# Twelve decay products, eight merge additions and 28 residual additions of a hybrid decoder layer, from GpSimd to DVE

## The chip, the cores and the metric

The kernel runs on one core of a Trainium2 chip. TensorE (PE in the profile) multiplies matrices, DVE is the vector engine, ScalarE (ACT) applies functions and copies, GpSimd (POOL) is a slower, programmable vector engine, and SyncE (SP) issues most DMAs. The metric is the device time in microseconds, from the median of several runs; one further execution was profiled.

## The reference

One layer of a decoder runs over 512 prompt rows and 32 sampled rows (8 sequences of 4). Cut to what the change touches:

```python
h = h + 0.5 * rmsnorm(swiglu(u, ffn1...), ffn1_post_g)          # residual addition behind a norm
z, xbc, dt, q, k, v, qi, ki, wi, g_ssd, g_att = split(rmsnorm(h) @ w_in)
...
decay  = exp(where(causal, a_cs[t] - a_cs[s], -inf))             # SSD, chunks of 128
cb     = einsum('bctgn,bcsgn->bctsg', cc, bc)                    # C B, one for a group of 4 heads
y_diag = einsum('bctsgr,bcsgrp->bctgrp', cb[..., None] * decay, xdt)
...
merged = sigmoid(g_ssd) * (y_ssd @ w_br_ssd) + sigmoid(g_att) * (y_att @ w_br_att)
h = h + rmsnorm(merged @ w_out, mix_post_g)                      # residual addition behind a norm
h = h + rmsnorm(mem_attend(rmsnorm(h)) @ w_mo, mem_post_g)       # the same
h = h + 0.5 * rmsnorm(swiglu(rmsnorm(h), ffn2...), ffn2_post_g)  # the same
```

There are 32 SSD heads in 8 groups, and the model width is 1024.

## The kernel before

All activations lie transposed: channels on the 128 partitions, 544 columns of tokens (512 prompt, 32 sample). A matrix product is made of three passes of fp32r (high by high, low by high, high by low; L310, accumulators `pg` and `pgh`), so every weight tile `wr` that lands is split by ScalarE into `wh` (L270) and by DVE into the rest `wl` (L271). The stages follow one another: ffn1, the mixing stage (first the indexer and the attention of the prompt, then the SSD groups 0 to 7 beside the selection and attention of the sample), the merge with w_out, the attention over the memory with w_mo, and ffn2. Side tasks are woven between the large products by hand (`weave`), and a scheduler of the build then puts each engine's instructions in order, so a change of one engine's work moves neighbours on others too.

Three places use GpSimd for an instruction with two full tensor operands:

- **SSD, `ssd_y`, L1380.** For each group and each half i (two heads), ScalarE turns the broadcast sums `abc` into decays (eight Relu of 128 columns, L1377, one Exp over 1024, L1379). Then `abc` is multiplied by `cb`, the masked C B that DVE has made from PSUM (L1353). GpSimd has this product, but for i = 1 in groups 1 to 4, where DVE has it: 12 on GpSimd, 4 on DVE. The products are read much later by `pY` (L1501). Around it DVE makes the convolution of the group that follows (`XO`, three multiply-adds L1326 and one L1329 for each of four tiles, whose inputs are in SBUF), `xd` and `xe` (L1368, L1370, from the transposes `pxt` in PSUM), and then a row of short ones (`cbs`, `xds`, `Gs`, `xef`, `Bs`).
- **Merge, L1761.** For each of eight output tiles m, DVE multiplies the accumulator by the gate (`gt`, L1760) and GpSimd adds the attention's part `y`. ScalarE then makes the high half `uh` and DVE the low half `ul` for w_out.
- **Norms, `bound`, L386.** Behind a norm, for each k of 8 tiles, DVE scales `y` (L385) and then `y` is added to the residual `hT`: on DVE for even k, on GpSimd for odd k. ScalarE squares the sum (L369), and GpSimd adds the square into `sqh` (L370; the last of eight is on DVE), from which TensorE makes the row sums `sth` for the norm that follows. `bound` runs for each half of the columns (256, 288) while the other half's products run; seven runs of it have a residual addition, so there are 28 such additions on GpSimd.

GpSimd also issues the gathers of the sampled attention (`kv`, L1618) and makes the low halves `wl` of the gates' weights.

Of the kernel before, what the change touches and what calls it, by code (L numbers as in the profile page):

```python
# [13 lines left out]
ALU = mybir.AluOpType  # L14
# [3 lines left out]
P = 128  # L18
T = 544
TP = 512  # L20
# [83 lines left out]
def weave(*gens, extra=(), loose=()):  # L104

    now, idle = 0.0, 0
    live = [[g, 0.0] for g in (*gens, *extra)]
    ends = [g for g in gens if g not in loose]  # L110
    while any(x[0] in ends for x in live):
        s = next((x for x in live if x[1] <= now), None)
        if s is None:
            s = min(live, key=lambda x: x[1])
            now = s[1]
        try:
            v = next(s[0])
        except StopIteration:
            live.remove(s)
            idle = 0  # L120
            continue
        if v is WAIT:
            idle += 1
            assert idle < 10000, "a wait that nothing ends"
            s[1] = now + 0.3
            continue
        idle = 0
        c, d = v if isinstance(v, tuple) else (v or 0.0, 0.0)
        now += c
        s[1] = now + d  # L130
# [38 lines left out]
class Net:  # L169
# [202 lines left out]
    def bound(self, half, sq, post_g, pre_g, rt=None):  # L372


        nc, hT, y = self.nc, self.hT, self.y
        r0, n = HALF[half]
        sl = slice(r0, r0 + n)
        if post_g is not None:
            yield 0.0, 3.0
            r = yield from self.rms_h(sq, half)  # L380
        if pre_g is not None:
            acc = self.nw.tile([P, 288], F32, tag="sqh", name="sqh", bufs=2)
        for k in range(8):
            if post_g is not None:
                nc.vector.scalar_tensor_tensor(y[:, k, sl], y[:, k, sl], post_g[:, k:k + 1], r, op0=ALU.mult, op1=ALU.mult)  # L385
                (nc.gpsimd if k % 2 else nc.vector).tensor_tensor(hT[:, k, sl], hT[:, k, sl], y[:, k, sl], op=ALU.add)  # L386
            if pre_g is not None:
                self.sq_acc(acc, hT[:, k, sl], n, k == 0, last=(k == 7))
            if rt is not None:
                g = pre_g[:, k:k + 1]  # L390
                nc.scalar.activation(self.uh[:, k, sl], hT[:, k, sl], AF.Copy, scale=g)
                nc.vector.scalar_tensor_tensor(self.ul[:, k, sl], hT[:, k, sl], g, self.uh[:, k, sl].bitcast(F32), op0=ALU.mult, op1=ALU.subtract)
            yield 0.0, 1.0
        if pre_g is None:
            return
        yield 0.0, 4.0 if rt is None else 8.0
        r = yield from self.rms_h(acc, half)
        if rt is not None:
            nc.scalar.copy(rt[:, sl], r)
            return  # L400
        for k in range(8):
            u = self.nw.tile([P, 288], F32, tag="u", name="u", bufs=2)
            nc.vector.scalar_tensor_tensor(u[:, :n], hT[:, k, sl], pre_g[:, k:k + 1], r, op0=ALU.mult, op1=ALU.mult)
            self.split(self.uh[:, k, sl], self.ul[:, k, sl], u[:, :n], nc.gpsimd if k % 4 == 3 else None)
            yield 0.0, 0.9
# [932 lines left out]
    def ssd_y(self, g, z):  # L1338
        nc, I, O, sp = self.nc, self.I, self.O, self.sp
# [3 lines left out]
        abc = []  # L1343
# [8 lines left out]
        cb = sp.tile([P, 4, P], F32, tag="cb", name="cb")  # L1352
# [20 lines left out]
        for i in range(2):  # L1373
            for h in range(2):
                for c in range(4):
                    col = c * 32 + 4 * g + 2 * i + h
                    nc.scalar.activation(abc[i][:, h, c * P:(c + 1) * P], abc[i][:, h, c * P:(c + 1) * P], AF.Relu, scale=-1.0,  # L1377
                                         bias=self.acs[:, col:col + 1])
            nc.scalar.activation(abc[i], abc[i], AF.Exp, scale=-1.0)  # L1379
            (nc.vector if 1 <= g <= 4 and i else nc.gpsimd).tensor_tensor(abc[i], abc[i], cb.rearrange("p c t -> p (c t)").unsqueeze(1).broadcast_to([P, 2, TP]), op=ALU.mult)  # L1380

        ps = self.ps1("pcs")
        for q in range(3):
# [106 lines left out]
        for i in range(2):  # L1490
# [14 lines left out]
            y = sp.tile([P, T], F32, tag=f"y{i}", name=f"y{i}")  # L1505
            nc.vector.scalar_tensor_tensor(y[:, :TP], XO[i][:, :TP], self.dsk[:, tl:tl + 1], ps, op0=ALU.mult, op1=ALU.add)
            nc.vector.tensor_tensor(y[:, P:TP], y[:, P:TP], E, op=ALU.add)
            t = sp.tile([P, 32], F32, tag="ty", name="ty")
# [229 lines left out]
    def merge(self, h_d, rest):  # L1738

        nc, I, y = self.nc, self.I, self.y  # L1740
        ex = ExitStack()
        ep = self.pool("mg", ex)
        ys = []

        def load():
            for k in range(16):
                yt = ep.tile([P, T], F32, tag="yt", name="yt", bufs=3)
                nc.sync.dma_start(yt, self.yssd_d[k])
                yh = ep.tile([P, T], F32R, name=f"yh{k}")
                yl = ep.tile([P, T], F32R, name=f"yl{k}")  # L1750
                self.split(yh, yl, yt)
                ys.append((yh, yl))
                yield 0.0, 2.0

        weave(rest, load())
        for m in range(8):
            w = self.weights(("w_br_ssd", m), [I["w_br_ssd"][0][:, m * P:(m + 1) * P]], 16)
            t = self.gate(0, m, ep)
            ps = result(self.mm(w, ys, 0))
            nc.vector.tensor_tensor(t, ps, t, op=ALU.mult)  # L1760
            nc.gpsimd.tensor_tensor(t, t, y[:, m, :], op=ALU.add)  # L1761
            self.split(self.uh[:, m, :], self.ul[:, m, :], t)
        ex.close()
        self.open_h()
        nc.sync.dma_start(self.hT, h_d.rearrange("k p t -> p k t"))
# [280 lines left out]
def result(gen):  # L2046

    while True:
        try:
            next(gen)  # L2050
        except StopIteration as e:
            return e.value
# [32 lines left out]
```

## Time and profile before

| | |
|---|---|
| median of 3 runs (lowest, highest) | 2201.06 us (2200.52, 2204.1) |
| the profiled execution, and its span | 2201.23 us, 2199.4 us |
| TensorE busy | 2101.4 us of the span |
| DVE, ScalarE, GpSimd busy | 1324.2, 955.2, 444.4 us |
| mean granted clock of TensorE | 0.979 |

The span runs from the first to the last instruction of the program. A busy time counts an instruction from its start to its end, also while it is held up. The granted clock is 1.0 where TensorE runs at 2.4 GHz and 0.5 where it runs at 1.2 GHz.

### The profile page before, as it was taken

The page shows a single profiled execution, that of the slowest core. Times are in us where ns is not written, and L with a number is a line of the kernel's source. Part 1 is how long each engine was busy: PE and PEld are TensorE (multiplying, and loading weights), DVE is VectorE, ACT ScalarE, POOL GpSimd, SP SyncE. Part 2 cuts the span into 40 slices and gives each one's busy share as a digit, 9 for nine tenths or more (in the row PEclk, how much of TensorE's full clock was granted, in tenths as well). Part 3 has the DMA queues.
Part 4 walks back from the last instruction along what each step waited for, and adds up shares of the span by engine and source line. Part 5 has one row for each costly group of instructions (what it writes and reads, how often), then busy time and mean ns, then how long its engine had stood idle before and what let it go on. Part 6 is the DMA issues. An engine that isn't in the chain of part 4 may idle for free.

```text
span 2199.4 us, 41232 instructions
## 1 busy us (share of the span) xinstructions
PE 2101.4 (96%) x16675; PEld 1960.6 (89%) x16675; DVE 1324.2 (60%) x2711; ACT 955.2 (43%) x1821; POOL 444.4 (20%) x461
## 2 busy tenths in 40 slices
PE   7999999999999999998999999999999979999998
PEld 7999999998788678897888889999987879999998
DVE  6543334475697989896677668544563475424455
ACT  6323345345445665453556445323535443222233
POOL 0000011032122302225555641012320320000011
PEclk9999999999999999998999999999999999999999
DMA  6424565347442223355456636564443433233243
GB/s 199 126 82 128 165 203 197 113 133 213 135 127 83 88 77 110 117 157 161 126 174 192 178 106 186 175 190 155 144 149 139 154 115 115 76 96 90 81 131 100
DMA packets 320107, 301.70 MB, mean 137 GB/s; under 512 B 25416, under 2 KB 290632, under 8 KB 318868
## 3 DMA queue, kind: packets, MB, share of 16 engines
q1 hardware_dynamic: 310508, 272.58, 40.5%
q0 software_dynamic: 8448, 25.18, 3.7%
q8 instruction: 131, 2.15, 0.4%
q10 hardware_dynamic: 960, 1.31, 0.2%
q14 instruction: 60, 0.49, 0.1%
HBM read 261.14 MB, written 37.35 MB: 136 GB/s over the span
## 4 chain that ended last, share of the span: by engine, by line
PE 72%; DVE 13%; DMA 6%; ACT 4%; issue 3%; POOL 2%; SPq 0%; DVEq 0%; ACTq 0%; POOLq 0%
PE pg L310 42%; PE pgh L310 14%; PE pmo L591 2%; DVE wl L271 2%; ACT wh L270 2%; DMA wr<-in_ffn_wu 1%; DVE gtm L1077 1%; DVE XO L1326 1%; DMA yt<-yssd_d 1%; DMA abc<-ac_d 1%; PE pmkT L1811 1%; POOL sqh L370 1%; PE pmo L1878 1%; DVE XO L1329 1%; DMA wr<-in_ffn_wg 1%
## 5 line engine op out<-in xcount | busy, mean ns | idle before, releaser
L270 ACT CAST wh<-wr 128x1024 fp32r<-128x1024 f32 (+3 forms) x362 | 341.6, 959 | 512.1 <-PE pg L310 288.2
L271 DVE TENSOR_TENSOR wl<-wr,wh 128x1024 fp32r<-128x1024 f32 (+3 forms) x338 | 391.1, 1171 | 222.6 <-ACT wh L270 215.8
L310 PE MATMUL pg<-uh,wh 128*128 128x256 f32 (+1 forms) x2336 | 504.1, 297 | 0.8 <-DVE zt L1291 0.8
L310 PE MATMUL pg<-ul,wh 128*128 128x256 f32 (+1 forms) x2336 | 493.4, 292 | 0.0
L310 PE MATMUL pg<-uh,wl 128*128 128x256 f32 (+1 forms) x2336 | 491.6, 291 | 0.0
L310 PEld LDWEIGHTS pg<-uh,wh 128*128 128x128 f32 x2336 | 380.4, 191 | 21.2 <-issue 17.2
L310 PEld LDWEIGHTS pg<-ul,wh 128*128 128x128 f32 x2336 | 381.2, 191 | 2.9 <-issue 2.2
L310 PEld LDWEIGHTS pg<-uh,wl 128*128 128x128 f32 x2336 | 380.0, 190 | 1.8 <-issue 1.4
L310 PE MATMUL pgh<-uh,wh 128*128 128x288 f32 (+2 forms) x880 | 260.8, 299 | 9.5 <-ACT wh L270 6.1
L310 PE MATMUL pgh<-uh,wl 128*128 128x256 f32 (+2 forms) x880 | 260.3, 298 | 7.3 <-DVE wl L271 7.3
L310 PE MATMUL pgh<-ul,wh 128*128 128x256 f32 (+1 forms) x880 | 257.1, 294 | 0.0
L310 PEld LDWEIGHTS pgh<-uh,wh 128*128 128x128 f32 (+1 forms) x880 | 170.4, 195 | 13.2 <-ACT wh L270 7.0
L310 PEld LDWEIGHTS pgh<-uh,wl 128*128 128x128 f32 (+1 forms) x880 | 169.5, 193 | 11.1 <-DVE wl L271 10.1
L310 PEld LDWEIGHTS pgh<-ul,wh 128*128 128x128 f32 x880 | 171.4, 195 | 0.9 <-issue 0.8
L370 POOL TENSOR_TENSOR sqf<-sqf,sqt 128x256 f32<-128x256 f32 (+1 forms) x48 | 52.4, 1092 | 508.9 <-ACT sqt L369 508.6
L310 PE MATMUL pgh<-hh,wh 128*128 128x288 f32 (+1 forms) x352 | 101.9, 290 | 0.0
L310 PE MATMUL pgh<-hh,wl 128*128 128x288 f32 (+1 forms) x352 | 101.2, 288 | 0.3 <-DVE wl L271 0.3
L310 PE MATMUL pgh<-hl,wh 128*128 128x288 f32 (+1 forms) x352 | 101.4, 288 | 0.0
L1326 DVE SCALAR_TENSOR_TENSOR XO<-CB,convw,XO 128x600 f32<-128x600 f32 x96 | 86.2, 899 | 7.1 <-ACT XO L1324 6.6
L702 POOL DMA_INDIRECT G<-in_cache_kidx,ix x16 | 16.4, 1025 | 361.7 <-DVE ix L697 281.2
L617 DVE TENSOR_TENSOR g<-pg,rt 128x544 f32<-128x544 f32 x32 | 23.2, 725 | 101.1 <-PE pg L310 101.1
L620 DVE TENSOR_TENSOR g<-pg,g 128x544 f32<-128x544 f32 x32 | 23.2, 725 | 99.1 <-PE pg L310 99.1
(608 smaller groups left out, 3875.4 us busy)
## 6 DMA issues: line engine op xcount, KB each, us to landing
wr<-in_w_in SPq DMA_DIRECT2D x66, 512.0 KB
wr<-in_ffn_wg SPq DMA_DIRECT2D x48, 512.0 KB
wr<-in_ffn_wu SPq DMA_DIRECT2D x48, 512.0 KB
wr<-in_ffn_wd SPq DMA_DIRECT2D x44, 384.0 KB
wr<-in_ffn_wd SPq DMA_DIRECT2D x44, 320.0 KB
kt_d<-KT SPq DMA_DIRECT2D x8, 1024.0 KB
KT<-kt_d SPq DMA_DIRECT2D x16, 512.0 KB
wr<-in_w_in SPq DMA_DIRECT2D x32, 256.0 KB
```

Source lines behind the costliest of these rows:

```text
L270: nc.scalar.copy(hi[:, s], r)
L271: (lo_eng or nc.vector).tensor_tensor(lo[:, s], r, hi[:, s].bitcast(F32), op=ALU.subtract)
L310: nc.tensor.matmul(o, a[:, k, c0:c0 + m], x[:, r0:r0 + n], start=(k == 0 and j == 0), stop=(k == KT - 1 and j == 2))
L370: (nc.vector if last else nc.gpsimd).tensor_tensor(acc[:, :n], acc[:, :n], s[:, :n], op=ALU.add)
L591: nc.tensor.matmul(ps[:, :256], a[:, k, i * P:(i + 1) * P], b[:, k, :], start=(k == 0 and j == 0), stop=(k == 7 and j == 2))
L617: nc.vector.tensor_tensor(g1[:, :n], pg, rt[:, sl], op=ALU.mult)
L620: nc.vector.tensor_tensor(g1[:, :n], pu, g1[:, :n], op=ALU.mult)
L1077: nc.vector.scalar_tensor_tensor(G, S, thr[:, j:j + 1], one, op0=ALU.is_ge, op1=ALU.mult, accum_out=cnt[:, j:j + 1])
L1326: nc.vector.scalar_tensor_tensor(xo, CB[:, j:j + 600], cw(j), xo, op0=ALU.mult, op1=ALU.add)
L1329: nc.vector.scalar_tensor_tensor(xo, th, 1.0, xo, op0=ALU.add, op1=ALU.mult)
L1811: nc.tensor.transpose(ps[:, (z * 2 + i) * P:(z * 2 + i + 1) * P], mk[:, i, (k + z) * P:(k + z + 1) * P], self.ident)
L1878: nc.tensor.matmul(ps[:, d * 256:(d + 1) * 256], mv[:, x, h * 256 + d * P:h * 256 + (d + 1) * P], PT[:, x, :], start=(x == 0), stop=(x == 1))
```

## The change

All 12 products, all 8 merge additions and all 28 residual additions of GpSimd are made by DVE. The operands, the arithmetic and the code's order are the same.

```diff
@@ -383,7 +383,7 @@
         for k in range(8):
             if post_g is not None:
                 nc.vector.scalar_tensor_tensor(y[:, k, sl], y[:, k, sl], post_g[:, k:k + 1], r, op0=ALU.mult, op1=ALU.mult)
-                (nc.gpsimd if k % 2 else nc.vector).tensor_tensor(hT[:, k, sl], hT[:, k, sl], y[:, k, sl], op=ALU.add)
+                nc.vector.tensor_tensor(hT[:, k, sl], hT[:, k, sl], y[:, k, sl], op=ALU.add)
@@ -1377,7 +1377,7 @@
             nc.scalar.activation(abc[i], abc[i], AF.Exp, scale=-1.0)
-            (nc.vector if 1 <= g <= 4 and i else nc.gpsimd).tensor_tensor(abc[i], abc[i], cb.rearrange("p c t -> p (c t)").unsqueeze(1).broadcast_to([P, 2, TP]), op=ALU.mult)
+            nc.vector.tensor_tensor(abc[i], abc[i], cb.rearrange("p c t -> p (c t)").unsqueeze(1).broadcast_to([P, 2, TP]), op=ALU.mult)
@@ -1758,7 +1758,7 @@
             nc.vector.tensor_tensor(t, ps, t, op=ALU.mult)
-            nc.gpsimd.tensor_tensor(t, t, y[:, m, :], op=ALU.add)
+            nc.vector.tensor_tensor(t, t, y[:, m, :], op=ALU.add)
```

Where they now stand in DVE's queue is decided by the build. DVE in SSD group 5, from the product `cb` on; `XO` is the convolution's tile of the group that follows, before:

```order
L1353 TENSOR_TENSOR cb<-pcb,tri 128x512
L1326 SCALAR_TENSOR_TENSOR XO_13366<-CB_8948,convw,XO_13366 128x600
L271 TENSOR_TENSOR wl<-wr,wh 128x1024
L1326 SCALAR_TENSOR_TENSOR XO_13366<-CB_8948,convw,XO_13366 128x600
L344 MEMSET nw 128x5
L1368 TENSOR_TENSOR xd<-pxt,dt 128x4x128
L1370 TENSOR_TENSOR xe<-pxt,te 128x4x128
L1329 SCALAR_TENSOR_TENSOR XO_13366<-th,XO_13366 128x600
L1291 SCALAR_TENSOR_TENSOR zt_13544<-zt_13544,pg 128x544
```

and after:

```order
L1353 TENSOR_TENSOR cb<-pcb,tri 128x512
L1326 SCALAR_TENSOR_TENSOR XO_13366<-CB_8948,convw,XO_13366 128x600
L1380 TENSOR_TENSOR abc<-abc,cb 128x1024
L1326 SCALAR_TENSOR_TENSOR XO_13366<-CB_8948,convw,XO_13366 128x600
L1380 TENSOR_TENSOR abc<-abc,cb 128x1024
L1329 SCALAR_TENSOR_TENSOR XO_13366<-th,XO_13366 128x600
L1368 TENSOR_TENSOR xd<-pxt,dt 128x4x128
L1370 TENSOR_TENSOR xe<-pxt,te 128x4x128
```

Both products stand ahead of L1329 now; the `wl` of the next weights, the memset and `zt` have moved behind.

DVE in SSD group 6, after the change, from the first L1326 behind `cb`; `PN` (L1677) is a copy for the sampled attention's `pO`:

```order
L1326 SCALAR_TENSOR_TENSOR XO_14210<-CB_8948,convw,XO_14210 128x600
L1675 COPY PZ<-pPT 128x8x4x8
L1326 SCALAR_TENSOR_TENSOR XO_14210<-CB_8948,convw,XO_14210 128x600
L1677 COPY PN<-pPT 32x128
L1326 SCALAR_TENSOR_TENSOR XO_14210<-CB_8948,convw,XO_14210 128x600
L1368 TENSOR_TENSOR xd<-pxt,dt 128x4x128
L1370 TENSOR_TENSOR xe<-pxt,te 128x4x128
L1329 SCALAR_TENSOR_TENSOR XO_14210<-th,XO_14210 128x600
L1380 TENSOR_TENSOR abc<-abc,cb 128x1024
```

Before, the rows down to L1329 stood in the same order, and `zt` where the first product stands now; the second one follows after the next `xd` and `xe`, ahead of `cbs`.

DVE at the end of the merge, as a piece of the difference (one of eight alike):

```order
 L1760 TENSOR_TENSOR gt<-pg,gt 128x544
-L271 TENSOR_TENSOR wl<-wr,wh 128x1024 x2
+L1761 TENSOR_TENSOR gt<-gt,y 128x544
+L271 TENSOR_TENSOR wl<-wr,wh 128x1024
 L319 TENSOR_TENSOR ul<-gt,uh 128x544
+L271 TENSOR_TENSOR wl<-wr,wh 128x1024
```

The addition stands directly behind its product, and one of two `wl` has gone behind `ul`.

## Rows read from the trace of the kernel before

**Rows 1.** The page: busy us (share of the span) and instructions by engine.
```profile
PE 2101.4 (96%) x16675; PEld 1960.6 (89%) x16675; DVE 1324.2 (60%) x2711; ACT 955.2 (43%) x1821; POOL 444.4 (20%) x461
```

**Rows 2.** Waits of TensorE: us in total, times, longest.
```profile
PE pxt L1367 <- DVE XO L1329: 10.4, 3, 5.3
PE sth L419 <- DVE sqh L370: 9.6, 3, 3.8
...
PE pO L1681 <- DVE PN L1677: 3.7, 1, 3.7
...
PE pmkT L1811 <- ACT y L1779: 2.1, 1, 2.1
```

**Rows 3.** Stretches: us; busy PE, PEld, DVE, ACT, POOL; PEclk, DMA share, GB/s.
```profile
850.00:1000.00 150.00, 138.06 (x1100) 128.62 (x1099) 137.73 (x271) 72.37 (x151) 34.97 (x43) 0.95 0.39 117
...
1220.00:1225.00 5.00, 5.00 (x31) 3.73 (x31) 3.22 (x12) 0.95 (x4) 2.83 (x3) 0.66 0.38 107
1285.00:1290.00 5.00, 4.15 (x31) 3.44 (x32) 3.34 (x6) 0.70 (x1) 2.07 (x3) 0.50 0.02 5
```

**Rows 4.** Single lines: ns least/median/most; and what ended idle time before L1380.
```profile
L386 DVE TENSOR_TENSOR hT<-hT,y x28: 409/453/1065, 461.9 to 2165.0; 128x256 f32<-128x256 f32 x16, 128x288 f32<-128x288 f32 x12
L386 POOL TENSOR_TENSOR hT<-hT,y x28: 741/920/1662, 462.1 to 2165.1; 128x256 f32<-128x256 f32 x16, 128x288 f32<-128x288 f32 x12
...
L1380 POOL TENSOR_TENSOR abc<-abc,cb x12: 2337/2391/3294, 858.5 to 1350.2; 128x1024 f32<-128x1024 f32 x12
...
L1380 DVE TENSOR_TENSOR abc<-abc,cb x4: 1216/1220/3226, 933.3 to 1149.8; 128x1024 f32<-128x1024 f32 x4
...
  DVE cb L1353: 22.0, 4
...
L1515 DVE TENSOR_TENSOR zt<-zt,zt x8: 718/724/729, 901.9 to 1381.7; 128x544 f32<-128x544 f32 x8
```

**Rows 5.** Timeline of GpSimd and DVE, SSD group 5: start, us.
```profile
1213.38 4.66 POOL L1380 TENSOR_TENSOR abc<-abc,cb 128x1024 f32<-128x1024 f32 x2
...
1213.43 5.26 DVE L1329 SCALAR_TENSOR_TENSOR XO<-th,XO 128x600 f32<-128x600 f32 x1
```

**Rows 6.** Timeline of GpSimd and DVE, SSD group 6.
```profile
1278.73 6.14 POOL L1380 TENSOR_TENSOR abc<-abc,cb 128x1024 f32<-128x1024 f32 x2 [0.92 <-DVE cb L1353]
...
1279.70 2.97 DVE L1326 SCALAR_TENSOR_TENSOR XO<-CB,convw,XO 128x600 f32<-128x600 f32 x1
...
1282.93 2.58 DVE L1326 SCALAR_TENSOR_TENSOR XO<-CB,convw,XO 128x600 f32<-128x600 f32 x1
...
1285.63 0.82 DVE L1326 SCALAR_TENSOR_TENSOR XO<-CB,convw,XO 128x600 f32<-128x600 f32 x1
...
1287.58 0.76 DVE L1329 SCALAR_TENSOR_TENSOR XO<-th,XO 128x600 f32<-128x600 f32 x1
```

**Rows 7.** Timeline of GpSimd and DVE, SSD group 2.
```profile
987.83 2.42 POOL L1380 TENSOR_TENSOR abc<-abc,cb 128x1024 f32<-128x1024 f32 x1
...
987.94 2.95 DVE L1326 SCALAR_TENSOR_TENSOR XO<-CB,convw,XO 128x600 f32<-128x600 f32 x1
```

**Rows 8.** Timeline of GpSimd and DVE, SSD group 1.
```profile
929.69 2.37 POOL L1380 TENSOR_TENSOR abc<-abc,cb 128x1024 f32<-128x1024 f32 x1 [11.13 <-DVE cb L1353]
...
930.92 0.69 DVE L1368 TENSOR_TENSOR xd<-pxt,dt 128x512 f32<-128x512 f32 x1 [1.31 <-PE pxt L1367]
```

**Rows 9.** Timeline at the end of the merge; in brackets idle time before, and releaser.
```profile
1522.04 3.50 DVE L271 TENSOR_TENSOR wl<-wr,wh 128x1024 fp32r<-128x1024 f32 x2
...
1522.07 2.39 POOL L1761 TENSOR_TENSOR gt<-gt,y 128x544 f32<-128x544 f32 x1 [9.55 <-ACT wh L270]
...
1525.19 0.51 PE L310 MATMUL pgh<-uh,wh 128*128 128x256 f32 x2 [1.54 <-ACT uh L318]
```

**Rows 10.** Timeline of GpSimd, norm after w_out, half 0.
```profile
1562.49 1.66 POOL L386 TENSOR_TENSOR hT<-hT,y 128x256 f32<-128x256 f32 x1 [1.54 <-DVE y L385]
...
1570.18 0.92 POOL L386 TENSOR_TENSOR hT<-hT,y 128x256 f32<-128x256 f32 x1
```

## The prediction

> **What bounds the kernel now.** I read the page first, then the waits of TensorE, then the DVE and GpSimd queues where it waits. The page shows TensorE busy for 2101.4 of 2199.4 us [rows 1]. No TensorE instruction changes, so no more is to be had than the 98 us in which it stands still, plus what the half clock after such stretches costs. The waits say where [rows 2]. The transposes `pxt` of the SSD branch wait three times, 10.4 us, for `XO` of DVE's line L1329. The row-sum matmuls `sth` of the norms wait three times, 9.6 us, for the last addition into `sqh`. `pO` of the sampled attention waits once, 3.7 us, for `PN`, and `pmkT` once, 2.1 us, for a copy by ScalarE inside the norm that follows w_out. All four stand behind DVE and GpSimd queues that the change touches. DVE is no idle engine: in 850 to 1000 us it is busy for 137.73 of 150 us [rows 3].
>
> **What moves, and at what price.** 48 instructions: 12 products `abc`, 28 additions `hT`, 8 additions `gt`. On GpSimd they take 2.39 and 0.92 us at the median, and the last `gt` 2.39; on DVE the first two forms take 1.22 and 0.45 (their least is 1.216 and 0.409), and for the third the nearest row is L1515, the same shape with both inputs in SBUF, 0.72 [rows 4, 9]. DVE gets 12 × 1.22 + 28 × 0.45 + 8 × 0.72 = 14.6 + 12.6 + 5.8 = 33.0 us of new work. DMAs, semaphores of other queues and ScalarE's work stay; GpSimd's own queue becomes shorter, so that the gathers `kv` behind `abc` are issued sooner.
>
> By itself that is a loss on an engine that is 92% busy in that stretch. The trace shows what is given back. In SSD group 5 DVE's L1329, which takes 0.76 us elsewhere [rows 6], takes 5.26 us: it starts at 1213.43, 0.05 us after GpSimd's two products began, and ends at 1218.7, when those 4.66 us are over [rows 5]. In group 6 two L1326 take 2.97 and 2.58 us where a third one takes 0.82 [rows 6]. In group 2 one takes 2.95 us beside a product [rows 7]. So a GpSimd product stops the DVE instruction that comes next, for as long as it lasts. In group 1 it does not: DVE's `xd` takes 0.69 us in the middle of GpSimd's 2.37 [rows 8]; its one full tensor besides a small factor comes from PSUM. There GpSimd's work was free.
>
> The Trainium skill, page "SBUF — State Buffer", section "Who interferes with whom", says that DVE and GpSimd have one port pair in common under an exclusive lock: a DVE instruction with two SBUF inputs and a GpSimd instruction that reads SBUF block each other for a whole instruction, and a DVE instruction with one SBUF input does not contend. The trace agrees on both sides, with 5.26 us for L1329 and 0.69 us for `xd`. By the rule the sum for DVE is a gain where the neighbour has two SBUF inputs and a loss of the whole product elsewhere; the rows, priced place by place below, come to the same signs.
>
> *SSD groups, gains.* Group 6: in the new order `PN` stands ahead of both products, so nothing delays it: 2.97 + 2.58 − 2 × 0.82 = 3.9 us earlier, which covers the wait of `pO`, 3.7 us [rows 2, 6]. Bounds 0 and 3.7; I take 3.7, since the place is read from the order. Group 5: the two products now stand ahead of L1329, and one `wl` that stood there goes behind (the same shape as a product, so the same 1.2 us): 5.26 − 0.76 = 4.5 us of lock goes, 2 × 1.22 − 1.2 = 1.2 comes, net 3.3 [rows 4, 5, 6]. Bounds 0 and 4.5. Group 2: 2.95 − 0.82 = 2.1 [rows 6, 7], bounds 0 and the longest wait of `pxt`, 5.3. Group 0 and 7 have two products each and locks too, and I count them as even. Sum 9.1 us.
>
> *SSD groups, losses.* Groups 1, 3 and 4 had one product on GpSimd each. It now stands on DVE ahead of `cbs`, `xds` and `Bs`, for which TensorE's next short matmuls wait. Bounds 0 (they wait for PSUM and have slack) and 1.22 each; I take the upper end, 3.7 us, because DVE has least slack there [rows 3], and leave out what locks come off there. I count no new wait for ScalarE's Exp: where GpSimd stood idle ahead of a product, `cb` ended it every time, 22.0 us in four [rows 4], and DVE makes `cb` itself. Net of the SSD: 9.1 − 3.7 = 5.4 us.
>
> *Norms.* Every boundary sends four of its eight `hT` additions through GpSimd, which also makes seven of the additions into `sqh`. In the one after w_out (half 0) GpSimd works almost without a gap from 1562.5 to 1571.1, its `hT` at 1562.49 takes 1.66 us, and its last one ends at 1571.1 [rows 10]; after that come ScalarE's square, the last `sqh` and `sth`. On DVE four of them are 4 × (0.92 − 0.45) = 1.9 us shorter [rows 4]. Four boundaries have TensorE waiting at their end (three `sth`, one `pmkT` [rows 2]): 4 × 1.9 = 7.5 us. Bounds: 0, if the next thing late is the weights' DMA or the remaining `sqh` additions, and 9.6 + 2.1 = 11.7, all of those waits. The first boundary (ffn1, half 0) waits for weights, and that of ffn2 is covered by TensorE's own work; both count nothing.
>
> *Merge.* Seven of eight `gt` additions are covered by the matmuls of the next m. The last is not: GpSimd takes 2.39 us, since DVE's `wl`, which started 0.03 us before, holds it up, and TensorE stands for 1.54 us on the way to w_out [rows 9]. In the new order the addition is on DVE directly behind its product and ahead of `wl`: 2.39 − 0.72 = 1.67, more than the wait, so 1.5 us. Bounds 0 and 1.54.
>
> *Clock.* After the waits in groups 5 and 6 the granted clock is 0.66 and 0.50 over five us each, that is 1.2 GHz for two thirds of the one and all of the other [rows 3]. Against 2.4 GHz this is (0.34 + 0.50) × 5 = 4.2 us of lost time. Bounds 0 and 4.2; I take half, 2.1. For the norms I take nothing.
>
> *Sum.* 5.4 + 7.5 + 1.5 + 2.1 = 16.5 us less. The profiled execution took 2201.23 us, span 2199.4; the median of the runs is 2201.06. 2201.2 − 16.5 = 2184.7, so 2185.
>
> **The rivals.**
> *A. Slower: DVE becomes what TensorE waits for in the SSD.* In groups 1 to 4 both moved product and the chain `xd`, `xe`, `cbs`, `xds`, `Bs` sit on DVE. Behind them the new order also puts `zt`, which empties a `pg` accumulator, two products and some ten short instructions later than before, and `wl`. For it: 137.73 of 150 us busy [rows 3]. Against it: DVE idles in the groups behind 1200 us, where half of the products are. Price: 12 × 1.22 = 14.6 us if every product were on TensorE's way and no lock came off; at two thirds of that, with the merge's 1.5 back, 2201 + 9.8 − 1.5 = 2209. It decides once the gains of groups 2, 5 and 6 (9.1) fall below what the twelve products add on the way, about eight of them. The Trainium skill's page "Perfetto Trace Analysis", section "Optimizing Scalar/DVE Operations", speaks for this rival: with a saturated DVE, offloading some work to GpSimd may make sense, though it adds that the two share a port and that it might not help. No run here shows that yet.
> *B. No difference: the waits only change their name.* At the norms the `sqh` additions stay on GpSimd and still lock DVE, and weights arrive late anyway; in groups 5 and 2 other DVE work fills the place. Then the merge (1.5) and a little of group 6 (2) are left: 2198.
> *C. More: all of it closes.* `sth`, `pmkT`, `pxt`, `pO`, merge and clock in full: 9.6 + 2.1 + 10.4 + 3.7 + 1.5 + 4.2 = 31.5, less 3.7: 27.8, so 2173. Against it: `pxt` waits in part for GpSimd's own `wl` of the gates, which stays.
>
> **How the numbers follow.** The forecast (2177 to 2193) gets 0.52: the locks are seen in rows, and the new order was read. C (below 2177) gets 0.16, B (2193 to 2204) 0.20, A 0.12. I put the range at 2170 to 2203, which leaves out A and the far end of C. A measurement of this kernel can tell about 0.2%, 4.4 us, from no change. A third of B lies below 2196.7, so faster 0.52 + 0.16 + 0.07 = 0.75, same 0.14, slower 0.11. The forecast's own range is 2177 to 2193.
>
> **What the new profile would show.** Right: GpSimd's busy time falls by some 74 us (12 × 2.39 + 28 × 0.92 + 8 × 2.4), no L1326 or L1329 over 2 us in groups 5 and 6, the 3.7 us of `pO` gone, `abc` on DVE at 1.22 each, `sth` waits below 6 us together, the merge's wait gone, and DVE's busy time up by clearly less than 33 us, for the locks are in its 1324 us of today. Wrong: DVE up by 25 us or more; new TensorE waits for `wl`, `zt` or `cbs` between 850 and 1200 us; `sth` waiting as long as before, with GpSimd's `sqh` or a DMA ahead of it; the half clock after 1215 and 1285 us still there.

## The result and the profile after

The changed kernel takes 2173.81 us (median of 4 runs, 2172.67 to 2174.79), the kernel before beside it 2200.89 (2200.52 to 2204.1): a ratio of 0.9874, 95% interval 0.9856 to 0.9891, 27.1 us less by the medians. The forecast was 16.5 us less, 2185, with a range of 2170 to 2203. Sign and range held, and the locks on which the forecast was built are gone. The size is that of rival C (27.8 us less), though not for C's reason: the waits for `sth` did not close.

The page of the kernel after, its row of busy times, answers to [rows 1]:

```profile
PE 2096.4 (96%) x16675; PEld 1955.8 (90%) x16675; DVE 1322.1 (61%) x2759; ACT 956.3 (44%) x1821; POOL 375.7 (17%) x413
```

This is the row to stop at. DVE has 48 instructions more and is busy 2.1 us **less**. The moved work takes 19.3 − 6.9 = 12.4 us (products), 30.2 − 18.2 = 12.0 (additions `hT`) and 5.8 (merge) on DVE in the two traces, 30.2 us together, so some 32 us came off DVE's other instructions. GpSimd is busy 68.7 us less (74 were forecast). TensorE's own busy time falls by 5.0 us with the same instructions: that is the clock (mean granted 0.983, before 0.979). The span falls from 2199.4 to 2172.9, 26.5 us, of which the remaining 21.5 were TensorE standing still.

The waits of TensorE in the kernel after (total, times, longest), answering to [rows 2]:

```profile
PE sth L419 <- DVE sqh L370: 8.6, 4, 3.5
...
PE pgh L310 <- DVE wl L271: 3.6, 6, 1.9
PE pg L310 <- DVE zt L1291: 3.2, 2, 2.7
...
PE pmkT L1811 <- ACT mkT__16911 L1812: 1.9, 1, 1.9
PE pg L310 <- DVE wl L271: 1.9, 1, 1.9
...
PE pxt L1367 <- DVE XO L1329: 0.6, 1, 0.6
```

`pxt` went from 10.4 us to 0.6, and `pO <- PN` (3.7) is gone. Two new waits stand in group 2: 1.88 us for `wl` at 982.85 us and 2.68 us for `zt` at 996.04. In the kernel before, 5.34 us of `pxt` stood there:

```profile
994.67 1.11 PE L1367 MATMUL pxt<-ident,XO 128*128 128x128 f32 x4 [5.34 <-DVE XO L1329]
```

`sth` hardly moved as a sum; it is taken apart below.

Stretches of the kernel after: the first is that of [rows 3]; the other two are the five us behind the start of `xd` of group 5 and behind L1329 of group 6 (columns as there).

```profile
850.00:1000.00 150.00, 140.05 (x1094) 129.30 (x1093) 136.46 (x278) 72.35 (x150) 27.14 (x36) 0.96 0.41 121
1206.00:1211.00 5.00, 5.00 (x46) 3.98 (x44) 4.91 (x13) 1.64 (x5) 3.92 (x6) 1.00 0.36 98
1270.00:1275.00 5.00, 5.00 (x43) 4.00 (x41) 4.96 (x9) 0.79 (x2) 4.09 (x4) 1.00 0.22 61
```

The granted clock behind groups 5 and 6 is 1.00, where it was 0.66 and 0.50 behind the two waits. In 850 to 1000 us DVE is no busier than before, though it makes six products there instead of two.

DVE's timeline of the kernel after, in group 5 (start, us), answering to [rows 5], and then in group 6, answering to [rows 6]:

```profile
1202.09 1.22 DVE L1380 TENSOR_TENSOR abc<-abc,cb 128x1024 f32<-128x1024 f32 x1
1203.22 0.89 DVE L1326 SCALAR_TENSOR_TENSOR XO<-CB,convw,XO 128x600 f32<-128x600 f32 x1
1204.04 1.21 DVE L1380 TENSOR_TENSOR abc<-abc,cb 128x1024 f32<-128x1024 f32 x1
1205.17 0.77 DVE L1329 SCALAR_TENSOR_TENSOR XO<-th,XO 128x600 f32<-128x600 f32 x1
...
1266.11 0.84 DVE L1326 SCALAR_TENSOR_TENSOR XO<-CB,convw,XO 128x600 f32<-128x600 f32 x1
...
1267.20 0.84 DVE L1326 SCALAR_TENSOR_TENSOR XO<-CB,convw,XO 128x600 f32<-128x600 f32 x1
1267.95 0.27 DVE L1677 COPY PN<-pPT 32x128 f32<-32x128 f32 x1
1268.15 0.82 DVE L1326 SCALAR_TENSOR_TENSOR XO<-CB,convw,XO 128x600 f32<-128x600 f32 x1
```

Both products of group 5 with the L1326 between them and L1329 are over in 3.9 us, less than the 5.26 us that L1329 alone took. In group 6 the two L1326 ahead of `PN` take 0.84 us each instead of 2.97 and 2.58.

Single lines of the kernel after (ns: least, median, most), answering to [rows 4]; L1329 took up to 5.26 us before:

```profile
L1380 DVE TENSOR_TENSOR abc<-abc,cb x16: 1205/1220/1235, 856.4 to 1331.5; 128x1024 f32<-128x1024 f32 x16
L386 DVE TENSOR_TENSOR hT<-hT,y x56: 409/447/1056, 461.1 to 2142.3; 128x256 f32<-128x256 f32 x32, 128x288 f32<-128x288 f32 x24
L1761 DVE TENSOR_TENSOR gt<-gt,y x8: 724/726/727, 1423.4 to 1501.5; 128x544 f32<-128x544 f32 x8
L1329 DVE SCALAR_TENSOR_TENSOR XO<-th,XO x32: 762/782/791, 836.9 to 1326.5; 128x600 f32<-128x600 f32 x32
```

The three prices of the forecast (1.22, 0.45, 0.72) stand.

### The profile page after: what moved, and what is told of

It reads as the page before. It is cut to its first block, busy times and chain, and to the rows that moved or that the text cites. A ratio compares the mean times of both kernels' runs of the same rounds, so it can differ in the third digit from the quotient of the medians.

```text
span 2172.9 us, 41213 instructions
## 1 busy us (share of the span) xinstructions
PE 2096.4 (96%) x16675; PEld 1955.8 (90%) x16675; DVE 1322.1 (61%) x2759; ACT 956.3 (44%) x1821; POOL 375.7 (17%) x413
## 4 chain that ended last, share of the span: by engine, by line
PE 76%; DVE 12%; DMA 4%; ACT 4%; issue 2%; POOL 1%; SPq 0%; DVEq 0%; ACTq 0%; POOLq 0%
PE pg L310 43%; PE pgh L310 17%; PE pmo L591 2%; DVE wl L271 2%; ACT wh L270 1%; DVE gtm L1077 1%; DMA wr<-in_ffn_wu 1%; DVE XO L1326 1%; DMA wr<-in_ffn_wg 1%; DMA yt<-yssd_d 1%; PE pY L1501 1%; PE pmkT L1811 1%; PE pmo L1878 1%; PE pkT L1644 1%; PE pms L1867 1%
## 5 line engine op out<-in xcount | busy, mean ns | idle before, releaser
L271 DVE TENSOR_TENSOR wl<-wr,wh 128x1024 fp32r<-128x1024 f32 (+3 forms) x338 | 376.8, 1126 | 212.4 <-ACT wh L270 209.0
L1326 DVE SCALAR_TENSOR_TENSOR XO<-CB,convw,XO 128x600 f32<-128x600 f32 x96 | 82.4, 860 | 4.2 <-ACT XO L1324 3.8
```

Of the source, the lines that this page charges most:

```text
L271: (lo_eng or nc.vector).tensor_tensor(lo[:, s], r, hi[:, s].bitcast(F32), op=ALU.subtract)
L1326: nc.vector.scalar_tensor_tensor(xo, CB[:, j:j + 600], cw(j), xo, op0=ALU.mult, op1=ALU.add)
```

## The experiments

They ran on chips on which the kernel before takes 2212 to 2217 us, 0.5 to 0.8% more than in the first comparison; every ratio is to the kernel before on the same chip, and the last column is (1 − ratio) times its median there. A ratio's interval is 0.0015 to 0.0025 to either side, 3 to 6 us.

| kernel | ratio | 95% interval | less than before |
|---|---|---|---|
| the 12 products alone | 0.9968 | 0.9952 to 0.9985 | 7.1 us |
| the 28 residual additions alone | 0.9955 | 0.9939 to 0.9970 | 10.0 |
| the 8 additions of the merge alone | 0.9995 | 0.9974 to 1.0017 | 1.1 |
| the changed kernel again | 0.9902 | 0.9884 to 0.9919 | 21.7 |
| changed, products of groups 5 to 7 back | 0.9951 | 0.9937 to 0.9965 | 10.9 |
| changed, 3 spare products of 256 columns | 0.9935 | 0.9911 to 0.9959 | 14.4 |
| changed, spare writes | 0.9905 | 0.9885 to 0.9925 | 21.1 |
| changed, 1 spare product of 768 columns | 0.9926 | 0.9910 to 0.9942 | 16.4 |
| changed, first product of groups 1, 3, 4 back | 0.9890 | 0.9874 to 0.9905 | 24.4 |
| changed, gates' `wl` on DVE | 0.9858 | 0.9840 to 0.9876 | 31.5 |
| changed, additions of squares on DVE | 0.9892 | 0.9869 to 0.9914 | 23.9 |
| changed, both of these on DVE | 0.9830 | 0.9813 to 0.9846 | 37.6 |

**The three parts alone.** Each is the kernel before with one line of the change's diff.

```diff
-            (nc.vector if 1 <= g <= 4 and i else nc.gpsimd).tensor_tensor(abc[i], abc[i], cb
+            nc.vector.tensor_tensor(abc[i], abc[i], cb
```

> The kernel before with the 12 decay products alone on DVE. Lock theory (a two-operand product of GpSimd stops the next DVE instruction that has two SBUF inputs): the two SSD steps that the changed kernel's matmuls show, 5.9 us around group 5 and 5.8 us around group 6, and the 2 to 3 us of the groups before, all come with this part: 13 to 16 us less than before, 2185 to 2188, and DVE's busy time stays within 5 us of 1324 although 14.6 us of products are added. Forecast's own term: 5.4 us less and 2.1 of the clock, 2193. Saturation theory (DVE is what TensorE waits for in groups 1 to 4): no gain or a loss, 2199 to 2209.

```diff
-                (nc.gpsimd if k % 2 else nc.vector).tensor_tensor(hT[:, k, sl], hT[:, k, sl], y[:, k, sl], op=ALU.add)
+                nc.vector.tensor_tensor(hT[:, k, sl], hT[:, k, sl], y[:, k, sl], op=ALU.add)
```

> The kernel before with the 28 residual additions alone on DVE. If the norms' gain is theirs: the changed kernel's matmuls show 3.4 us less at the norm after w_out half 0, 2.1 at half 1, 2.0 and then minus 1.4 at the two after w_mo: 6 to 7.5 us less than before, about 2194 to 2195. If the boundary norms only gain because the SSD groups ahead of them let the weights come sooner, this part alone gives nothing: 2200 to 2201.

```diff
-            nc.gpsimd.tensor_tensor(t, t, y[:, m, :], op=ALU.add)
+            nc.vector.tensor_tensor(t, t, y[:, m, :], op=ALU.add)
```

> The kernel before with the eight additions of the merge alone on DVE. The last one held TensorE for 1.54 us ahead of w_out, so 1.4 to 1.5 us less, 2199.5, if nothing else moves; 2201 if the next late thing (DVE's split of the same tile) takes the wait over. GpSimd's busy time falls by about 19 us (8 times 2.4) and DVE's busy time rises by less than the 5.8 us of its new work, since some of the locked instructions beside those additions become short.

Measured: 7.1, 10.0 and 1.1 us less, together 18.2. The products came to half of what the steps of the first pair of traces had promised (13 to 16), and to the forecast's 5.4 + 2.1; the norms to more. DVE's busy time is 1317.8 us with the products alone (14.6 us of work added, 6.4 less in all), 1330.3 with the residual additions (6.1 more), 1318.1 with the merge's (6.1 less, 5.8 added). So the products take 21 us of other work off DVE, the merge's additions 12 and the residual additions 6.5, half of what they cost it. These busy times, each of one execution, don't add up: the parts make 6.4 us less, and the changed kernel shows 2.1.

**The control.** The changed kernel unaltered.

> The changed kernel itself once more, as the measure for the parts: they were timed on chips on which the kernel before takes 2215 to 2217 us, 0.7% more than where the change was first timed (2200.9). Parts that add up: 0.9968, 0.9955 and 0.9995 make 0.9918, some 18 us less than before. The first timing carried over: 0.9874, some 28 us less, and then 9 to 10 us come only with the parts together.

Measured: 0.9902, beside 0.9918 for the product of the three parts: within the intervals the parts add up, with no sign of a gain that needs them together. What is left over is between the first comparison (27 us) and this one (22), and their intervals just overlap. The traces show where it lies. TensorE and ScalarE in the control:

```profile
1089.98 0.37 ACT L1416 COPY H<-pst 128x256 f32<-128x256 f32 x1 [6.94 <-remote]
...
1090.41 1.22 PE L1413 MATMUL pst<-xe,Bt 128*128 128x256 f32 x2 [3.81 <-ACT H L1416]
```

ScalarE stood for 6.94 us ahead of the copy `H`, and TensorE for 3.81 us behind it. The view calls the releaser `remote` because it finds no instruction that ends where the wait ends. The semaphore is TensorE's own: matmuls that end, as modelled, between 1085.6 and 1086.6 us have their four updates of it together at 1089.92 to 1090.04. In each of the twelve traces of the experiments 70 to 76 of TensorE's some 1335 updates have no record within 0.3 us of the end of their matmul, all but one of them between 994 and 1319 us, the stretch of the gathers `kv`. In the two traces of the first comparison there is none. The kernels with the residual additions or the merge's additions alone, which leave the SSD as it was, have them too (76 and 71), so they do not come from the moved products. But ScalarE stands at most 1.1 us for such an update in those two kernels and up to 12.1 us in the ones with moved products, so whether the change makes them dearer stays open. What delays them, no run here shows.

That stretch is also where time is lost against the first comparison. The kernel with the merge's additions alone has the same instructions up to there as the kernel before; between 1050 and 1215 us its matmuls go from 2.8 us ahead of the first trace of the kernel before to 5.9 us behind, some 8.6 us; with the residual additions alone it is 10.2. The control loses 12.8 us there against the first trace of the changed kernel. So 27 and 22 us are measured under two conditions, and 2.6 to 4.2 of the 5 us between them lie in this stretch, by one execution of each kernel.

**Products of groups 5, 6 and 7 back on GpSimd.**

```diff
-            nc.vector.tensor_tensor(abc[i], abc[i], cb
+            (nc.gpsimd if g >= 5 else nc.vector).tensor_tensor(abc[i], abc[i], cb
```

> The changed kernel with the products of groups 5, 6 and 7 (both halves) back on GpSimd. If the two steps of 5.9 and 5.8 us around groups 5 and 6 are theirs: 9 to 12 us slower than the changed kernel, 2183 to 2186, with pxt's and pO's waits back. If they come from a queue that moved earlier in the program: within 2 us of 2174.

Measured: 10.9 us less than before instead of 21.7. These six instructions are worth 11 us, as the two steps said (5.9 and 5.8 us, named in the expectation for the products alone). TensorE's waits in this kernel (total, times, longest):

```profile
PE pO L1681 <- DVE PN L1677: 4.8, 2, 3.8
PE pxt L1367 <- DVE XO L1329: 4.6, 2, 4.0
```

L1329 in this kernel (ns: least, median, most):

```profile
L1329 DVE SCALAR_TENSOR_TENSOR XO<-th,XO x32: 760/783/5260, 842.2 to 1363.3; 128x600 f32<-128x600 f32 x32
```

Neither `PN` nor `XO` reads a product. They are late because the instructions ahead of them are held up, and the 5.26 us are back to the hundredth.

**What holds DVE up: reading, writing, or GpSimd's queue.** Three kernels do unused work on GpSimd at the 12 places, beside the changed kernel's product on DVE; nothing of the reference is left out. The first makes three products over 256 columns, the second the same length of time mostly in memsets (seven of 0.31 us), the third one product over 768 columns, which it writes as bf16 where the first writes float32.

```diff
+ [nc.gpsimd.tensor_tensor(jk, cb[:, 0:2, :].rearrange("p c t -> p (c t)"), cb[:, 2:4, :].rearrange("p c t -> p (c t)"), op=ALU.mult) for c in range(0 if 1 <= g <= 4 and i else 3)]
```

> The changed kernel, and beside each of the 12 products GpSimd makes three unused two-operand products of 128x256 from the same tile cb: some 2.2 us each place, 26 us in all, that no result waits for. Lock theory: DVE's next instructions with two SBUF inputs (L1326, L1329, the splits) are held up again, DVE's busy time rises by 15 us or more, and 6 to 15 us of the SSD's gain go: 2180 to 2189. Queue theory (the gain was that GpSimd's queue became free for its gathers and splits): the same loss as the next kernel, which fills the queue as long with instructions that don't read, except for 28 columns of them. Order theory (the gain was only DVE's new order): no loss in either, 2174.

```diff
+ [nc.gpsimd.memset(jk, 0.0) if c else nc.gpsimd.tensor_copy(jk[:, :4], cb[:, 0, :4]) for c in range(0 if 1 <= g <= 4 and i else 8)]
```

> The changed kernel, and beside each of the 12 products GpSimd makes a copy of four columns of cb and seven unused memsets of 128x256: some 2.2 us each place, as long as the three products of the kernel before this one, but nearly all of it only writes. Lock theory: DVE's instructions beside them stay as short as in the changed kernel, DVE's busy time within 5 us of 1322, time 2174 to 2177. Queue theory: as much slower as the kernel with the spare products. The two kernels beside each other are the test: the lock says 6 us or more between them, the queue says none.

```diff
+ [nc.gpsimd.tensor_tensor(jk, cb.rearrange("p c t -> p (c t)")[:, :384].unsqueeze(1).broadcast_to([P, 2, 384]), cb.rearrange("p c t -> p (c t)")[:, 128:].unsqueeze(1).broadcast_to([P, 2, 384]), op=ALU.mult) for c in range(0 if 1 <= g <= 4 and i else 1)]
```

> The changed kernel, and at the same 12 places one unused two-operand product of GpSimd over 768 columns of cb, in place of the three products over 256 (0.74 us each) of the earlier kernel, which raised DVE's busy time by 5.2 us only and held no DVE instruction for more than 0.54 us besides one. If DVE waits for the end of the GpSimd instruction that runs, the length of one instruction sets the price: single holds of 1 to 2 us, DVE's busy time at least 8 us above that of the kernel with the write-only work (1320.8), ratio to before 0.993 to 0.996. If the two engines share by turns, whatever the length: holds of 0.5 us again, DVE 1326, ratio 0.9935 as with three short ones. If only GpSimd's queue counts: 0.990, as with the write-only work.

Group 6 in the kernel with the long product; the last row is TensorE's:

```profile
1281.60 5.05 POOL L1380 TENSOR_TENSOR jk<-cb 128x768 bf16<-128x768 f32 x2 [0.57 <-DVE cb L1353]
1282.57 2.42 DVE L1326 SCALAR_TENSOR_TENSOR XO<-CB,convw,XO 128x600 f32<-128x600 f32 x1
...
1285.25 2.04 DVE L1326 SCALAR_TENSOR_TENSOR XO<-CB,convw,XO 128x600 f32<-128x600 f32 x1
1287.22 0.27 DVE L1677 COPY PN<-pPT 32x128 f32<-32x128 f32 x1
...
1287.63 0.43 PE L1681 MATMUL pO<-vs,PN 32*64 32x128 f32 x4 [2.62 <-DVE PN L1677]
```

and in the kernel with the writes:

```profile
1281.87 0.83 DVE L1326 SCALAR_TENSOR_TENSOR XO<-CB,convw,XO 128x600 f32<-128x600 f32 x1
1282.05 2.52 POOL L1380 MEMSET jk<- 128x256 f32 x7
1282.95 0.83 DVE L1326 SCALAR_TENSOR_TENSOR XO<-CB,convw,XO 128x600 f32<-128x600 f32 x1
```

The same DVE instruction takes 2.42 us beside a GpSimd product and 0.83 beside memsets that go on as long. DVE's busy time is 1320.8 us with the writes, 1326.0 with three short products (5.2 more, a third of the 15 that were expected) and 1330.7 with one long one (9.9 more). The longest excess of a DVE instruction over its usual time was 0.54 us beside short products and 1.62 beside long ones (leaving out one in each that stood beside a gates' `wl` too). So what counts is that GpSimd reads, and the length of a single instruction of it; the share-by-turns theory falls. A single write as long as a product was not tried. The writes cost no time that can be measured (0.9905 beside 0.9902), so a free GpSimd queue was not the gain. In time the two kernels with products lie 5 to 7 us above the control, with intervals that overlap its own. For the short products this is no clean price of the lock: 3.1 us of it is a single wait of `pO`, from 1231.0 us, for a gather `kv` that stood in GpSimd's queue behind spare work (1220.6 to 1225.4 us).

The Trainium skill, page "SBUF — State Buffer", section "Who interferes with whom", says this: a DVE instruction with two SBUF inputs contends with a GpSimd instruction that reads SBUF, not with one that only writes it. The 2.42 and 0.83 us agree.

**Was anything lost in groups 1, 3 and 4?** The first product of these three groups goes back to GpSimd.

```diff
+            (nc.gpsimd if g in (1, 3, 4) and i == 0 else nc.vector).tensor_tensor(abc[i], abc[i], cb
```

> The changed kernel with the first product of groups 1, 3 and 4 back on GpSimd, the three places that the forecast priced as losses of 1.22 us each. Forecast's term: 3.7 us faster than the changed kernel, 2170. Lock theory without such a loss: 0 to 2 us slower, 2174 to 2176, since the locked DVE instructions there cost what the product does. The new TensorE waits of the changed kernel at 982.85 us (for wl) and 996.04 us (for zt) go in the first case.

Measured: 0.9890 beside 0.9902, 2.7 us faster by the medians, with overlapping intervals: it doesn't tell 3.7 from 0. The wait for `zt`, 2.8 us at most in this kernel, stays, so these three products did not make it; that for `wl` goes from 1.9 us to 1.3.

**The same step further.** The gates' `wl`, then the additions of squares in the norms, then both go to DVE.

```diff
-                w = self.win((C_GS, C_GA)[x] + c * 256, lo_eng=self.nc.gpsimd)
+                w = self.win((C_GS, C_GA)[x] + c * 256)
```

> The changed kernel with the gates' low halves wl (24 subtractions of 128x8x256 that are left on GpSimd) on DVE as well. Lock theory carried on: they hold up DVE by some 19 us in the trace, against 24 times 1.22 = 29 us of new work on DVE, which still has slack there: 3 to 8 us faster, 2166 to 2171. Saturation: the gates fill DVE's queue and TensorE waits for wl of its next weights: 2178 to 2190.

```diff
-            (nc.vector if last else nc.gpsimd).tensor_tensor(acc[:, :n], acc[:, :n], s[:, :n], op=ALU.add)
+            nc.vector.tensor_tensor(acc[:, :n], acc[:, :n], s[:, :n], op=ALU.add)
```

> The changed kernel with the additions of squares (L370, 84 of them on GpSimd, 0.92 to 1.27 us each) on DVE as well, 0.45 us each as the residual additions. They hold up DVE by some 24 us in the trace of the changed kernel, so DVE's busy time stays within 10 us of 1322. Lock and chain theory: the four sth waits (8.6 us) shrink below 5 and the time falls by 3 to 8 us. Rival: each square now queues on DVE behind the next scaling of y and ScalarE's square is what is late: within 2 us of the changed kernel. Saturation: slower by 3 or more.

> The changed kernel with the 16 low halves wl of the gates and all additions of squares on DVE: nothing of GpSimd is left beside the norms and the gates but single-input work and gathers. If the two edits work in stretches of their own, as their traces say (gates 640 to 960 us, norms elsewhere), their gains add: 4 to 10 us below the changed kernel. If the norms lose with the squares on DVE: slower than the kernel with the gates' wl alone (ratio 0.9858 to before).

Measured: the gates' `wl` give another 9.8 us beside the control (0.9858, intervals apart), more than expected, and 16 of the 24 subtractions are the gates', not all. L1326 and L271 of the kernel with the gates' `wl` on DVE:

```profile
L1326 DVE SCALAR_TENSOR_TENSOR XO<-CB,convw,XO x96: 821/839/884, 823.2 to 1328.9; 128x600 f32<-128x600 f32 x96
...
L271 POOL TENSOR_TENSOR wl<-wr,wh x8: 2346/2408/2585, 550.8 to 643.3; 128x1024 fp32r<-128x1024 f32 x8
```

No L1326 is above 0.884 us any more (2.955 in the changed kernel). DVE is busy 1318.0 us, 4 less than in the changed kernel, with 19.5 us of work added.

The squares alone give nothing that can be measured (0.9892 beside 0.9902; 1.5 us by the medians), although the theory's sign came: `sth` fell to 2.2 us, and DVE's busy time rose by 6 only. TensorE's waits in the control:

```profile
PE sth L419 <- DVE sqh L370: 8.7, 4, 3.5
...
PE pgh L310 <- ACT wh L270: 5.3, 4, 3.4
PE pgh L310 <- DVE wl L271: 4.8, 9, 1.9
```

and with the squares on DVE:

```profile
PE pgh L310 <- ACT wh L270: 7.8, 5, 3.4
PE pgh L310 <- DVE wl L271: 6.6, 8, 2.5
...
PE sth L419 <- DVE sqh L370: 2.2, 2, 2.0
```

Of the 6.5 us that `sth` lost, 4.3 came back as waits for the halves of the next weights: the time is the one that the rival expected (within 2 us). Both together take 2174.23 us where the control takes 2190.83 on the same chip, more than the 4 to 10 us that were expected: this version beats both kernels.

## Why the prediction was right, and where its sizes were off

TensorE's idle time between the same places of the first pair of traces, beside the forecast's terms:

| where | forecast, us less | measured, us less |
|---|---|---|
| ahead of the SSD (to 860 us) | 0 | 1.8 |
| SSD groups | 5.4 | 12.7 |
| merge | 1.5 | 1.5 |
| norms behind it | 7.5 | 5.0 |
| clock (TensorE's busy time) | 2.1 | 5.0 |
| sum | 16.5 | 26.0 of 26.5 |

**Gains of groups 5, 6 and 2.** Right in kind. Group 5's `pxt` wait, 4.03 us, and group 6's `pO`, 3.70, are gone whole. With the late products back on GpSimd both return. With the long spare product, in the changed kernel's order of DVE, 2.62 us of `pO` return beside two held L1326, which shows the lock as the cause in group 6. In group 5 the spare products ran beside `xd` and `xe` (1216.0 to 1219.9 us), and `pxt` did not wait; there the lock is shown by L1329's 5.26 us beside GpSimd's products, in a run in which DVE's order went back too. The forecast read that L1329 ends when the two products are over; they end at 1218.04 us [rows 5] and L1329 0.65 us later, which is about its own length and leaves the 4.5 us of lock as they were. Group 2 failed by its own rival B: 5.34 us of `pxt` became 1.88 and 2.68 us for `wl` and `zt`, a net 0.8 for the 2.1 that were forecast. These are also the new waits that rival A and the signs of being wrong named; they remained that small.

**Losses of groups 1, 3 and 4.** By the two traces this is the largest miss: 3.7 us were charged, and the idle time there fell by 2.7. That term took the upper bound because DVE had no slack by its busy share, and it said that it leaves out the locks that come off there. But some 6 of those 137.73 us were locks: with four products more (4.9 us) they became 136.46. Part of the 2.7 is a `psr` wait in group 3, which varies between 0.6 and 3.0 us over the kernels here whether or not group 3's products are on DVE, so a gain there is not shown. Nor is a loss ruled out: timed, the products alone (7.1 us) give less than the last six of them (10.9), and putting these three back gave 2.7 us. Both lean towards the loss that was charged, neither beyond its interval, so the sign of this term stays open.

**Groups 0 and 7, counted as even,** gave 2.3 us: three small waits gave 0.5, 0.9 and 0.9. Groups 0 to 7 make 13.5 together so; small waits that grew take 0.8 back.

**Merge.** 1.54 us of wait gone, as forecast, by the trace; the timed part alone (1.1 us, −3.8 to 5.8) can't confirm it.

**Norms.** By the waits the step was right three times: `sth` after w_out half 1 fell from 3.81 to 1.72 us, after w_mo half 0 from 3.63 to 1.84, and `pmkT` with the wait right behind it from 3.73 to 1.93: 2.1, 1.8 and 1.8 for a forecast of 1.9 each. The fourth (ffn1 half 1) gave 0.6, from 2.16 to 1.60. Against it, `sth` after w_mo half 1 is new, 3.50 us, where 4.03 us of waits for weights had stood (1.49 and 2.54): a changed name, worth nothing. That is why the sum of `sth`, which was to fall below 6, is 8.6 although three of its waits shrank; as a sign it was badly chosen. The timed part, 10.0 us (6.6 to 13.5), holds the term of 7.5.

**Clock.** The forecast took only half of its 4.2 us, and the clock is at its upper level behind both waits now. Over the whole span TensorE's busy time fell by 5.0 us. Some of this is not the change: stretches at 1.2 GHz at 629 and 831 us, where nothing was moved, are missing in the trace after, and the kernel with the merge's additions alone is 4.3 us ahead of the kernel before by its matmuls at 840 us, without any change up to there.

**What stays open:** 27 us in the first comparison and 22 in the second, 5 us above the forecast. That the range was met is safe for both; which of the two sizes the change has depends on what delays the semaphores beside the gathers, and that is not known. The forecast's own 16.5 came from terms that missed in both directions (7.5 for the norms against 5.0, 5.4 for the SSD against 12.7), so its distance from either figure is partly luck.

## What to carry to other kernels

Before an engine is called full, look in its queue for instructions that take several times their least duration, and at what GpSimd does in those moments: DVE's 1324 us of busy time hid 32 us of being held up, and giving it 30 us of work from GpSimd cost it nothing. Leave GpSimd what only writes, or what stands beside DVE work that reads PSUM; a long two-operand product of GpSimd is paid by whichever DVE instruction with two inputs in SBUF comes next, and by all that queue behind that one. Count a wait as gained only when the next late thing is known: `sth` gave 6.5 us and the weights took back 4.3.

## What was not expected of the hardware

A product of GpSimd over 768 columns held DVE's next instruction for up to 1.62 us, three over 256 columns for up to 0.54, for the same work: length of a single instruction sets the hold. The hold goes the other way too: GpSimd's spare product took 0.74 us at the median and up to 1.72, its long one 1.84 and up to 2.74. The long times stand beside DVE instructions with both inputs in SBUF; beside `xd` and `xe` alone the two took 0.73 and 1.82. And in the later executions updates of TensorE's semaphore come late in the stretch of the gathers, so that ScalarE stands up to 12.1 us for one (6.94 in the control, 7.3 with the products alone, none in the first pair), at a cost of 2.4 to 3.8 us to TensorE where `pst` needs the copy `H`; their cause is open.
